# Row maxima one step later, reciprocals two steps behind the scores, and low parts and half sums late in a step: an attention block on one core

## The chip, the cores and the metric

The kernel runs on one core of one Trainium2 chip. The metric is device time in microseconds. The kernel before was timed in three runs, with a median of 973.12 us (972.27 to 975.09).

## The reference

One layer of a streaming encoder, for a sequence of 1024 rows with 1024 features, all in float32. Two attention branches with 8 heads each share one input projection; each branch's output is gated, projected, merged with a sigmoid gate and sent through an output projection. The heart of each branch is the same: scores, a causal mask, softmax over the keys, times V.

```python
# branch A, 8 heads: 64 features + 32 rotary features, mask by chunks of 64 keys
for i in range(seq // Q_BLOCK):               # Q_BLOCK = 128 rows
    lo, hi = i * Q_BLOCK, (i + 1) * Q_BLOCK
    s = (q_nope[lo:hi] . k_nope[:hi] + q_rope[lo:hi] . k_rope[:hi]) * scale
    s = jnp.where(chunk_causal_mask(lo, hi), s, -jnp.inf)
    p = jax.nn.softmax(s, axis=-1)
    outs.append(p @ v[:hi])
# branch B, 8 heads of 64: the same with cum[lo:hi] - cum[:hi] added, mask by single keys
y_a = o_a * jax.nn.silu(gate_a)
y_b = o_b * jax.nn.silu(gate_b)
merged = (sigmoid(mg_a) * (y_a @ w_branch_a) + sigmoid(mg_b) * (y_b @ w_branch_b))
x = x + gate * (merged @ w_out)
```

## The kernel before

The kernel is one program with a written order for each engine; nothing reorders it at run time. A float32 product is made of a high part (float32r, by a cast on ScalarE) and a low part (the difference, by VectorE), so each matmul is three or two passes over high and low operands. This is why so much of VectorE's work is subtraction: of P, of weights, of Q and K.

The first 260 us project the input. Then comes `attention()`, from about 286 to 816 us: 16 heads, eight of branch A and eight of branch B, each in 12 steps of nominally 2.49 us (`STEP`). Step k of a head is one pair (g, j): g is the half of the 1024 queries (4 row tiles of 128 each), j the tile of 128 keys; k below 4 is (0, k), the others are (1, k - 4). In a step:

- `turn` transposes the blocks of the normalised P that belong to keys j into a "t" bank of PSUM (two buffers). ScalarE copies the high part out of it, VectorE subtracts the low part (`pp` in the traces).
- ScalarE computes the exp of the score tile that was made a step ago (`p_h` for a tile of the first half, `p_u` for one of the second).
- In some steps (0, 3, 5, 6 and 10 of even heads, 3 of odd ones) Q or K of the next two heads is transposed into a "t" bank (`qt`, `kt`) and written as high and low operands (`prep_a`, `prep_b`).
- `scores` makes the scores of row tile i of a coming head (the table `ahead` says which), in bank "n" for i below 4 and bank "s" for the others. Each has one buffer. VectorE puts the mask on (a memset of a 64 x 64 corner in branch A, an addition in branch B) and takes the negated row maximum `nm`.
- VectorE takes the reciprocal `rs` of the sum of the last exp, and GpSimd multiplies P by it.
- `fill_to` issues matmuls of an independent product, the gates' projections of the input (`f` in the traces), until the step has its length. Their evacuation (a tanh on ScalarE, a combined add and multiply on VectorE, `gate`) and the splitting of the next weights (two casts on ScalarE, two low parts `lo_f` on VectorE) are issued where the fill comes to them. Then the products P V of the last step (`o`), and after a head's half the two halves of o are added (`op`), gated on GpSimd and stored.

So each engine's queue is a list, and the code's order in a step is the order in each queue. Once, at step 0 of head 3, `gate_row` adds `gcol` on VectorE, and PE transposes it at once (`pgT`).

The order of issue in a step of the kernel before:

```python
pr = self.turn(n, g, j)              # transposes, high part, low part
if last: next(last)                  # exp of the last score tile
if (n, k) in parts: next(preps[parts[n, k]])
if k in ahead and ...: finish = self.scores(...)   # scores, mask, row maximum
if last: next(last)                  # reciprocal, multiply
...
self.fill_to(due - 600)              # fill, and its evacuations
```

Of the kernel before, what the change touches and what calls it, by code (L numbers as in the profile page):

```python
# [10 lines left out]
F32 = mybir.dt.float32  # L11
# [4 lines left out]
ALU = mybir.AluOpType  # L16
# [3 lines left out]
P = 128  # L20
# [54 lines left out]
class Net:  # L75
# [954 lines left out]
    def prep_a(self, n):  # L1030

        nc, U = self.nc, self.U
        h = self.seq[n][1]
        cols = slice(h * 64, h * 64 + P)
        ops = {}

        def load(nm, dram):
            src = U.get([P, ST, P], F32, f"{nm}s{n}")
            nc.sync.dma_start(src, dram[:, :, cols].rearrange("s p d -> p s d"))
            return src  # L1040

        def operands(nm):
            for e in range(2):
                ops[nm, e] = U.get([P, S], F32R, f"{nm}1_{n + e}"), U.get([P, S], F32R, f"{nm}2_{n + e}")
                r = (h + e) % 4 * 32
                for j, x in enumerate(ops[nm, e]):
                    nc.sync.dma_start(x[64:96].bitcast(F32),
                                      self.qr_d[j, (h + e) // 4, r:r + 32] if nm == "q" else self.kr_d[j])

        def group(nm, src, vec, g):  # L1050
            pt = self.bank("t", f"{nm}t{n}{g}")
            for i in range(4):
                self.transpose(pt[:, i * P:(i + 1) * P], src[:, g * 4 + i])
            sl = slice(g * 512, (g + 1) * 512)
            own = (slice(0, 64), slice(64, 128))
            for e in range(2):
                nc.scalar.activation(ops[nm, e][0][0:64, sl], pt[own[e]], AF.Copy, scale=vec[own[e]])
            for e in range(2):
                nc.vector.scalar_tensor_tensor(out=ops[nm, e][1][0:64, sl], in0=pt[own[e]], scalar=vec[own[e]],
                                               in1=ops[nm, e][0][0:64, sl].bitcast(F32), op0=ALU.mult, op1=ALU.subtract)  # L1060
            if g == 1:
                U.put(src)

        src = load("q", self.qa_d)
        yield
        operands("q")
        group("q", src, self.vqa, 0)
        yield
        group("q", src, self.vqa, 1)
        yield  # L1070
        src = load("k", self.ka_d)
        yield
        operands("k")
        group("k", src, self.vka, 0)
        for e in range(2):
            self.qk[n + e] = [*ops["q", e], *ops["k", e]]
            qh, ql, kh, kl = (x[0:96] for x in self.qk[n + e])
            self.passes[n + e] = [(qh, kh), (qh, kl), (ql, kh)]
        yield
        group("k", src, self.vka, 1)  # L1080
        yield

    def prep_b(self, n):
# [17 lines left out]
        def group(nm, src, vec, g):  # L1101
            pt = self.bank("t", f"{nm}t{n}{g}")
            for i in range(4):
                self.transpose(pt[:, i * P:(i + 1) * P], src[:, g * 4 + i])
            sl = slice(g * 512, (g + 1) * 512)
            own = (slice(0, 64), slice(64, 128))
            for e in range(2):
                nc.scalar.activation(x1[nm, e][own[e], sl], pt[own[e]], AF.Copy, scale=vec[own[e]])
            for e in range(2):
                hi = x1[nm, e][own[e], sl].bitcast(F32)  # L1110

                lo, again = (x2[nm, e][0:64, sl], x1[nm, e][own[1 - e], sl])[::1 if nm == "q" else -1]
                nc.vector.scalar_tensor_tensor(out=lo, in0=pt[own[e]], scalar=vec[own[e]], in1=hi,
                                               op0=ALU.mult, op1=ALU.subtract)
                nc.gpsimd.tensor_scalar(out=again, in0=hi, scalar1=1.0, scalar2=0.0, op0=ALU.mult, op1=ALU.add)
            if g == 1:
                U.put(src)

# [24 lines left out]
    def scores(self, n, i):  # L1143
# [14 lines left out]
        if i == 7:  # L1158
            self.U.put(*self.qk.pop(n))
        sv = s[:, base:base + w]  # L1160
        if br == "b":
            nc.vector.tensor_tensor(out=sv[:, w - P:w], in0=sv[:, w - P:w], in1=self.maskb, op=ALU.add)
        else:
            nc.vector.memset(sv[0:64, w - 64:w], NEG)
        nm = pa.tile([P, 1], F32, tag="nm", bufs=4, name=f"nm{n}_{i}")
        nc.vector.tensor_reduce(out=nm, in_=sv, axis=AX.X, op=ALU.max, negate=True)  # L1166
        p = self.Hs.get([P, 512], F32, f"p{n}_{i}") if i < 4 else self.U.get([P, S], F32, f"p{n}_{i}")
        self.p[n, i] = p

        def finish():  # L1170
            sm = pa.tile([P, 1], F32, tag="sm", bufs=4, name=f"sm{n}_{i}")
            nc.scalar.activation(p[:, 0:w], sv, AF.Exp, bias=nm, accum_out=sm)  # L1172
            yield
            rs = pa.tile([P, 1], F32, tag="rs", bufs=4, name=f"rs{n}_{i}")
            nc.vector.reciprocal(rs, sm)  # L1175
            nc.gpsimd.tensor_scalar(out=p[:, 0:w], in0=p[:, 0:w], scalar1=rs, scalar2=0.0, op0=ALU.mult, op1=ALU.add)  # L1176
            yield
        return finish()

    def turn(self, n, g, j):  # L1180
# [9 lines left out]
        pp = self.U.get([P, 2, 512], F32R, f"pp{n}_{g}{j}")  # L1190
        ph, pl = pp[:, 0], pp[:, 1]
        nc.scalar.copy(ph[:, c0:], pt[:, c0:])  # L1192
        nc.vector.tensor_tensor(out=pl[:, c0:], in0=pt[:, c0:], in1=ph[:, c0:].bitcast(F32), op=ALU.subtract)  # L1193

        def product():
            v = self.v[n]
# [13 lines left out]
            nc.scalar.copy(tmp[0:64], o[64:128])  # L1210
            if n % 2 == 0 and g == 0:
                self.opair = self.U.get([P, S], F32, f"op{n}")
            r0 = (n % 2) * 64
            sl = slice(g * 512, (g + 1) * 512)
            op = self.opair[:, sl]
# [2 lines left out]
            if n % 2 == 1:  # L1218
# [9 lines left out]
                else:  # L1228
# [5 lines left out]
                        nc.scalar.copy(hi[:, sl], op)  # L1234
                        nc.vector.tensor_tensor(out=lo[:, sl], in0=op, in1=hi[:, sl].bitcast(F32), op=ALU.subtract)
                    self.U.put(self.opair, gate)
        return product

    def attention(self):
        N = len(self.seq)  # L1240
# [14 lines left out]
        for c, i in enumerate((0, 4, 1, 5, 2, 3, 6)):  # L1255
            if c == 3:
                self.load_v(1)
            if c == 4:
                while not self.g1b_done:
                    next(self.fill)  # L1260
                self.fbanks = "fg"
            if finish:
                next(finish)
            f = self.scores(0, i)
            if finish:
                next(finish)
            finish = f
            self.fill_to(self.pe_time + 1500)
        due = self.pe_time
        ahead = {1: (0, 7), 2: (1, 0), 4: (1, 1), 6: (1, 2), 8: (1, 3), 7: (1, 4), 9: (1, 5), 11: (1, 6)}  # L1270
        for n in range(N):
            for k in range(12):
                g, j = (0, k) if k < 4 else (1, k - 4)
                due += self.STEP
                pr = self.turn(n, g, j)
                last, finish = finish, None
                if last:
                    next(last)
                if (n, k) in parts:
                    next(preps[parts[n, k]])  # L1280
                if k in ahead and n + ahead[k][0] < N:
                    finish = self.scores(n + ahead[k][0], ahead[k][1])
                if last:
                    next(last)
                if k == 2 and 0 < n < N - 1:
                    self.load_v(n + 1)
                for at, call, a in self.extra:
# [46 lines left out]
    def build(self):  # L1334
# [26 lines left out]
        self.pending, self.pending_b = (), ()  # L1361
        self.seq = [("a", h) for h in range(H)] + [("b", h) for h in range(H)]
        self.passes, self.qk, self.v, self.p, self.gates, self.y, self.wo = {}, {}, {}, {}, {}, {}, {}
        self.extra = []
        for k in range(2):
            self.extra += [((14, 1), self.load_y, (0, k)), ((14, 3), self.split_y, (0, k)),
                           ((14, 4), self.load_y, (0, 2 + k)), ((14, 6 + k), self.split_y, (0, 2 + k)),
# [127 lines left out]
```

## Time and profile before

| | |
|---|---|
| median of three runs | 973.12 us (972.27 to 975.09) |
| profiled execution | 970.98 us, of which the span is 969.0 |
| TensorE busy | 952.2 us (98%) |
| VectorE busy | 636.0 us (66%) |
| ScalarE busy | 477.6 us (49%) |
| GpSimd busy | 204.0 us (21%) |
| DMA | 39.3% of 16 engines' span, 124 MB |

The share of TensorE says that there is next to no time in which it does not work; the share of the others says that they have time on the whole, but not at which moment. TensorE's clock is the other thing to read: the profile gives the clock granted to it, 1.00 for 2.4 GHz and 0.50 for 1.2 GHz. How the engines' queues meet has to be read from the timeline of single steps.

### The profile page before, as it was taken

The page shows a single profiled execution, that of the slowest core. Times are in us where ns is not written, and L with a number is a line of the kernel's source. Part 1 is how long each engine was busy: PE and PEld are TensorE (multiplying, and loading weights), DVE is VectorE, ACT ScalarE, POOL GpSimd, SP SyncE. Part 2 cuts the span into 40 slices and gives each one's busy share as a digit, 9 for nine tenths or more (in the row PEclk, how much of TensorE's full clock was granted, in tenths as well). Part 3 has the DMA queues.
Part 4 walks back from the last instruction along what each step waited for, and adds up shares of the span by engine and source line. Part 5 has one row for each costly group of instructions (what it writes and reads, how often), then busy time and mean ns, then how long its engine had stood idle before and what let it go on. Part 6 is the DMA issues. An engine that isn't in the chain of part 4 may idle for free.

```text
span 969.0 us, 15332 instructions
## 1 busy us (share of the span) xinstructions
PE 952.2 (98%) x5582; PEld 832.3 (86%) x5582; DVE 636.0 (66%) x1379; ACT 477.6 (49%) x959; POOL 204.0 (21%) x260
## 2 busy tenths in 40 slices
PE   7999999999999999999999999999999999999998
PEld 7999999999988888788888888888888878887887
DVE  3967977787646667567667676677676766596222
ACT  7776634443245656546555566465655644143000
POOL 0022132200011222122233233232332220045000
PEclk9999999999999999999999999999999999999999
DMA  9821132864943224225232232322411554633321
GB/s 348 322 95 45 50 116 81 295 225 169 312 134 98 87 67 131 66 74 155 79 109 67 66 90 67 114 85 88 132 56 44 185 185 153 245 141 125 109 88 66
DMA packets 80987, 124.99 MB, mean 129 GB/s; under 512 B 5928, under 2 KB 47536, under 8 KB 80912
## 3 DMA queue, kind: packets, MB, share of 16 engines
q1 hardware_dynamic: 80912, 124.01, 39.3%
q8 instruction: 44, 0.72, 0.3%
q14 instruction: 31, 0.25, 0.1%
HBM read 88.33 MB, written 35.66 MB: 128 GB/s over the span
## 4 chain that ended last, share of the span: by engine, by line
PE 89%; DVE 4%; DMA 3%; ACT 2%; issue 2%; POOL 0%; SPq 0%; ACTq 0%; DVEq 0%
PE f L127 31%; PE b L127 12%; PE out L127 9%; PE s L127 9%; PE o L127 7%; PE pt L136 6%; PE q L127 3%; PE ckv L127 2%; PE kv L127 2%; PE cq_s L127 2%; DVE hT_lo L998 1%; DMA ks_u<-ka_d 1%; PE cq_t L127 1%; DVE mg_h L991 1%; PE pada L127 1%
## 5 line engine op out<-in xcount | busy, mean ns | idle before, releaser
L1192 ACT CAST pp_u<-pt 128x512 fp32r<-128x512 f32 x192 | 92.2, 480 | 178.9 <-PE pt L136 164.9
L1193 DVE TENSOR_TENSOR pp_u<-pt,pp_u 128x512 fp32r<-128x512 f32 x192 | 106.5, 555 | 76.5 <-ACT pp_u L1192 74.4
L127 PE MATMUL f<-hT_hi,hi_f_u 128*128 128x512 f32 x384 | 153.9, 401 | 0.0
L127 PE MATMUL f<-hT_lo,hi_f_u 128*128 128x512 f32 x384 | 153.7, 400 | 0.0
L127 PE MATMUL f<-hT_hi,lo_f_u 128*128 128x512 f32 x384 | 153.5, 400 | 0.0
L127 PE MATMUL s<-k_u,q_u 96*128 96x512 f32 (+6 forms) x480 | 117.1, 363 | 1.2 <-ACT p_h L1172 0.7
L127 PE MATMUL b<-hi_b_u,hT_hi 128*128 128x256 f32 x384 | 109.6, 286 | 0.0
L127 PE MATMUL b<-hi_b_u,hT_lo 128*128 128x256 f32 x384 | 108.6, 283 | 0.0
L127 PE MATMUL b<-lo_b_u,hT_hi 128*128 128x256 f32 x384 | 108.6, 283 | 0.0
L1176 POOL TENSOR_SCALAR p_u<-p_u,rs 128x640 f32<-128x640 f32 (+1 forms) x64 | 64.7, 1011 | 169.1 <-DVE rs L1175 93.2
L1166 DVE TENSOR_REDUCE nm<-s 128x1 f32<-128x128 f32 (+7 forms) x128 | 97.0, 758 | 4.4
L127 PE MATMUL o<-pp_u,v_u 128*128 128x512 f32 (+7 forms) x384 | 94.4, 340 | 0.0
L1176 POOL TENSOR_SCALAR p_h<-p_h,rs 128x128 f32<-128x128 f32 (+1 forms) x64 | 36.9, 577 | 249.3 <-DVE rs L1175 220.0
L127 PEld LDWEIGHTS s<-k_u,q_u 96*128 96x128 f32 (+2 forms) x480 | 77.1, 191 | 7.0 <-ACT p_h L1172 1.2
L127 PEld LDWEIGHTS f<-hT_hi,lo_f_u 128*128 128x128 f32 x384 | 72.5, 189 | 12.0
L127 PEld LDWEIGHTS f<-hT_hi,hi_f_u 128*128 128x128 f32 x384 | 72.7, 189 | 11.1
L127 PEld LDWEIGHTS f<-hT_lo,hi_f_u 128*128 128x128 f32 x384 | 72.5, 189 | 11.2
L127 PEld LDWEIGHTS o<-pp_u,v_u 128*128 128x128 f32 (+1 forms) x384 | 62.0, 162 | 19.7 <-issue 0.2
L127 PEld LDWEIGHTS b<-lo_b_u,hT_hi 128*128 128x128 f32 x384 | 73.6, 192 | 0.3
L127 PEld LDWEIGHTS b<-hi_b_u,hT_hi 128*128 128x128 f32 x384 | 73.6, 192 | 0.3
L127 PEld LDWEIGHTS b<-hi_b_u,hT_lo 128*128 128x128 f32 x384 | 73.6, 192 | 0.0
L136 PEld LDWEIGHTS pt<-ident,p_u 128*128 128x128 f32 x416 | 52.7, 140 | 16.7
(310 smaller groups left out, 1998.5 us busy)
## 6 DMA issues: line engine op xcount, KB each, us to landing
raw_f_u<-in_w_t SPq DMA_DIRECT2D x24, 512.0 KB
wada_u<-in_w_ada SPq DMA_DIRECT2D x16, 512.0 KB
mg_d<-th_h SPq DMA_DIRECT2D x32, 256.0 KB
mg_h<-mg_d SPq DMA_DIRECT2D x32, 256.0 KB
raw_b_u<-in_w_b SPq DMA_DIRECT2D x12, 512.0 KB
x_u<-in_x SPq DMA_DIRECT2D x8, 512.0 KB
raw_wg_u<-in_w_gate SPq DMA_DIRECT2D x8, 512.0 KB
va_d<-vhl_u SPq DMA_DIRECT2D x8, 512.0 KB
```

Source lines behind the costliest of these rows:

```text
L127: self.nc.tensor.matmul(out, lhsT=l, rhs=r, start=start, stop=stop)
L136: self.nc.tensor.transpose(out=out, in_=in_, identity=self.ident)
L991: nc.vector.scalar_tensor_tensor(out=m, in0=m, scalar=1.0, in1=acc, op0=ALU.add, op1=ALU.mult)
L998: nc.vector.tensor_tensor(out=self.hT_lo[x], in0=mA[c1][:, x[2]], in1=self.hT_hi[x].bitcast(F32), op=ALU.subtract)
L1166: nc.vector.tensor_reduce(out=nm, in_=sv, axis=AX.X, op=ALU.max, negate=True)
L1176: nc.gpsimd.tensor_scalar(out=p[:, 0:w], in0=p[:, 0:w], scalar1=rs, scalar2=0.0, op0=ALU.mult, op1=ALU.add)
L1192: nc.scalar.copy(ph[:, c0:], pt[:, c0:])
L1193: nc.vector.tensor_tensor(out=pl[:, c0:], in0=pt[:, c0:], in1=ph[:, c0:].bitcast(F32), op=ALU.subtract)
```

## The change

Three of the pieces of VectorE's work in a step move. The mask and the row maximum go from `scores` to the beginning of the next step, ahead of that step's low part of P. The reciprocal and GpSimd's multiply go two steps behind the scores. The low parts of the operands of later heads (and GpSimd's copies with them) and the sum of the halves of o are collected in a list, `late`, and issued behind the reciprocal, the latter one step after its product.

```diff
@@ prep_a (prep_b alike, with its copies on GpSimd)
-            for e in range(2):
-                nc.vector.scalar_tensor_tensor(out=ops[nm, e][1][0:64, sl], in0=pt[own[e]], scalar=vec[own[e]],
-                                               in1=ops[nm, e][0][0:64, sl].bitcast(F32), op0=ALU.mult, op1=ALU.subtract)
+
+            def lows():
+                for e in range(2):
+                    nc.vector.scalar_tensor_tensor(out=ops[nm, e][1][0:64, sl], in0=pt[own[e]], scalar=vec[own[e]],
+                                                   in1=ops[nm, e][0][0:64, sl].bitcast(F32), op0=ALU.mult, op1=ALU.subtract)
+
+            if n == 0:
+                lows()
+            else:
+                self.late.append(lows)
...
@@ scores
         sv = s[:, base:base + w]
-        if br == "b":
-            nc.vector.tensor_tensor(out=sv[:, w - P:w], in0=sv[:, w - P:w], in1=self.maskb, op=ALU.add)
-        else:
-            nc.vector.memset(sv[0:64, w - 64:w], NEG)
-        nm = pa.tile([P, 1], F32, tag="nm", bufs=4, name=f"nm{n}_{i}")
-        nc.vector.tensor_reduce(out=nm, in_=sv, axis=AX.X, op=ALU.max, negate=True)
...
         def finish():
+            if br == "b":
+                nc.vector.tensor_tensor(out=sv[:, w - P:w], in0=sv[:, w - P:w], in1=self.maskb, op=ALU.add)
+            else:
+                nc.vector.memset(sv[0:64, w - 64:w], NEG)
+            nm = pa.tile([P, 1], F32, tag="nm", bufs=4, name=f"nm{n}_{i}")
+            nc.vector.tensor_reduce(out=nm, in_=sv, axis=AX.X, op=ALU.max, negate=True)
+            yield
             sm = pa.tile([P, 1], F32, tag="sm", bufs=4, name=f"sm{n}_{i}")
             nc.scalar.activation(p[:, 0:w], sv, AF.Exp, bias=nm, accum_out=sm)
             yield
@@ turn
-        nc.vector.tensor_tensor(out=pl[:, c0:], in0=pt[:, c0:], in1=ph[:, c0:].bitcast(F32), op=ALU.subtract)
+
+        def low():
+            nc.vector.tensor_tensor(out=pl[:, c0:], in0=pt[:, c0:], in1=ph[:, c0:].bitcast(F32), op=ALU.subtract)
...
+            if n < 15:
+                self.late.append(lambda: collect(o, tmp))
+            else:
+                collect(o, tmp)
+
+        def collect(o, tmp):
             r0 = (n % 2) * 64
...
-        return product
+        return low, product
@@ attention
+        last, opening = None, True
         for n in range(N):
             for k in range(12):
                 g, j = (0, k) if k < 4 else (1, k - 4)
                 due += self.STEP
-                pr = self.turn(n, g, j)
-                last, finish = finish, None
+                older, last, finish = last, finish, None
+                if last and not opening:
+                    next(last)
+                low, pr = self.turn(n, g, j)
+                low()
                 if last:
                     next(last)
                 if (n, k) in parts:
                     next(preps[parts[n, k]])
                 if k in ahead and n + ahead[k][0] < N:
                     finish = self.scores(n + ahead[k][0], ahead[k][1])
-                if last:
-                    next(last)
+                if older:
+                    next(older)
+                opening = False
+                while self.late:
+                    self.late.pop(0)()
```

What this does to the queues: the order on PE, ACT, POOL and SP is the same in both kernels, and on DVE it changes throughout the attention. Three places show how. In the names, `pp7_17` is the part of P of head 7 for half 1 and key tile 7, `s8_6` and `nm8_6` the scores and the row maximum of tile 6 of head 8, `rs8_5` a reciprocal, `lo_f13` the low parts of a weight of the fill, `gate4` an evacuation of the fill. The numbers behind them are buffers.

The first place is VectorE's queue at the end of head 7 and the first two steps of head 8, in the kernel before:

```order
L1175 RECIPROCAL rs8_5_6478<-sm8_5_6476 128x1
L1193 TENSOR_TENSOR pp7_17_u26_386_6494<-pt7_17_6492,pp7_17_u26_386_6494 128x128
L1162 TENSOR_TENSOR s8_6_6497<-s8_6_6497,maskb_105 128x128
L1166 TENSOR_REDUCE nm8_6_6503<-s8_6_6497 128x1
L978 SCALAR_TENSOR_TENSOR gate4_u8_388_6512<-th120_h0_142_6510,f12_00_6433 128x512
L116 TENSOR_TENSOR lo_f13_u23_390_6515<-raw_f13_u27_382_6431,hi_f13_u7_389_6514 128x512 x2
L1193 TENSOR_TENSOR pp8_00_u28_391_6531<-pt8_00_6526,pp8_00_u28_391_6531 128x512
L1175 RECIPROCAL rs8_6_6538<-sm8_6_6534 128x1
```

The same place in the changed kernel:

```order
L1207 TENSOR_TENSOR pp7_17_u21_386_6491<-pt7_17_6489,pp7_17_u21_386_6491 128x128
L1187 RECIPROCAL rs8_5_6500<-sm8_5_6473 128x1
L978 SCALAR_TENSOR_TENSOR gate4_u8_388_6509<-th120_h0_142_6507,f12_00_6427 128x512
L116 TENSOR_TENSOR lo_f13_u23_390_6512<-raw_f13_u27_382_6425,hi_f13_u7_389_6511 128x512 x2
L1177 TENSOR_TENSOR s8_6_6494<-s8_6_6494,maskb_105 128x128
L1181 TENSOR_REDUCE nm8_6_6524<-s8_6_6494 128x1
L1207 TENSOR_TENSOR pp8_00_u28_391_6531<-pt8_00_6526,pp8_00_u28_391_6531 128x512
L1207 TENSOR_TENSOR pp8_01_u2_393_6555<-pt8_01_6551,pp8_01_u2_393_6555 128x384
```

Mask and row maximum of tile 6 stood ahead of the fill's gate and low parts and now stand behind them; the reciprocal of tile 5 went behind the low part of its step.

The second place is VectorE's queue in steps 8 to 10 of head 9, in the kernel before:

```order
L1162 TENSOR_TENSOR s10_3_7144<-s10_3_7144,maskb_105 128x128
L1166 TENSOR_REDUCE nm10_3_7148<-s10_3_7144 128x1
L1175 RECIPROCAL rs10_4_7151<-sm10_4_7142 128x1
L978 SCALAR_TENSOR_TENSOR gate5_u13_438_7164<-th150_h7_160_7162,f15_00_7071 128x512
L1193 TENSOR_TENSOR pp9_15_u3_439_7170<-pt9_15_7166,pp9_15_u3_439_7170 128x384
L1162 TENSOR_TENSOR s10_5_7175<-s10_5_7175,maskb_105 128x128
L1166 TENSOR_REDUCE nm10_5_7181<-s10_5_7175 128x1
L1175 RECIPROCAL rs10_3_7184<-sm10_3_7173 128x1
L116 TENSOR_TENSOR lo_f16_u10_442_7188<-raw_f16_u14_433_7069,hi_f16_u28_441_7187 128x512 x2
L1193 TENSOR_TENSOR pp9_16_u16_443_7204<-pt9_16_7201,pp9_16_u16_443_7204 128x256
L1175 RECIPROCAL rs10_5_7209<-sm10_5_7207 128x1
```

The same place in the changed kernel:

```order
L978 SCALAR_TENSOR_TENSOR gate5_u3_438_7158<-th150_h2_160_7156,f15_00_7068 128x512
L1177 TENSOR_TENSOR s10_3_7141<-s10_3_7141,maskb_105 128x128
L1181 TENSOR_REDUCE nm10_3_7161<-s10_3_7141 128x1
L1207 TENSOR_TENSOR pp9_15_u1_439_7167<-pt9_15_7163,pp9_15_u1_439_7167 128x384
L1187 RECIPROCAL rs10_4_7178<-sm10_4_7139 128x1
L116 TENSOR_TENSOR lo_f16_u18_442_7182<-raw_f16_u14_433_7066,hi_f16_u28_441_7181 128x512 x2
L1177 TENSOR_TENSOR s10_5_7172<-s10_5_7172,maskb_105 128x128
L1181 TENSOR_REDUCE nm10_5_7196<-s10_5_7172 128x1
L1207 TENSOR_TENSOR pp9_16_u10_443_7201<-pt9_16_7198,pp9_16_u10_443_7201 128x256
L1187 RECIPROCAL rs10_3_7206<-sm10_3_7170 128x1
```

The row maximum of tile 3 went behind the gate, that of tile 5 behind the pair of low parts of the weight f16.

The third place is VectorE's queue at step 0 of head 3, where `gate_row` is, in the kernel before:

```order
L1193 TENSOR_TENSOR pp2_17_u9_255_4704<-pt2_17_4702,pp2_17_u9_255_4704 128x128
L1164 MEMSET s3_6_4707 64x64
L1166 TENSOR_REDUCE nm3_6_4715<-s3_6_4707 128x1
L1193 TENSOR_TENSOR pp3_00_u6_257_4729<-pt3_00_4724,pp3_00_u6_257_4729 128x512
L1175 RECIPROCAL rs3_6_4734<-sm3_6_4732 128x1
L897 TENSOR_TENSOR gcol_113<-gcol_113,vec_91 128x8
```

The same place in the changed kernel:

```order
L1207 TENSOR_TENSOR pp2_17_u9_255_4701<-pt2_17_4699,pp2_17_u9_255_4701 128x128
L1187 RECIPROCAL rs3_5_4712<-sm3_5_4667 128x1
L1179 MEMSET s3_6_4704 64x64
L1181 TENSOR_REDUCE nm3_6_4722<-s3_6_4704 128x1
L1207 TENSOR_TENSOR pp3_00_u6_257_4729<-pt3_00_4724,pp3_00_u6_257_4729 128x512
L897 TENSOR_TENSOR gcol_113<-gcol_113,vec_91 128x8
```

The reciprocal of tile 6 is no longer in front of `gcol`; that of tile 5 comes in its place, ahead of the row maximum.

## Rows read from the trace of the kernel before

**Rows 1.** The page: busy us and share of the span of each engine.

```profile
PE 952.2 (98%) x5582; PEld 832.3 (86%) x5582; DVE 636.0 (66%) x1379; ACT 477.6 (49%) x959; POOL 204.0 (21%) x260
```

**Rows 2.** Waits of PE, 300 to 816 us: us in total, times, longest.

```profile
PE pgT L136 <- DVE gcol L897: 2.4, 1, 2.4
PE s L127 <- ACT p_u L1172: 0.5, 1, 0.5
PE qt L136 <- DVE pp_u L1193: 0.2, 1, 0.2
```

**Rows 3.** Windows: busy us (count) PE, PEld, DVE, ACT, POOL; PEclk; DMA; GB/s.

```profile
395.50:398.91 3.41, 3.41 (x13) 2.61 (x12) 0.74 (x2) 1.66 (x3) 0.00 (x0) 0.50 0.87 214
875.00:885.00 10.00, 8.32 (x38) 6.55 (x37) 7.98 (x12) 6.01 (x11) 4.35 (x4) 1.00 0.30 109
```

**Rows 4.** Timeline (start us, length us, engine), heads 7 and 8, 555 to 560.

```profile
555.42 1.09 DVE L1166 TENSOR_REDUCE nm<-s 128x1 f32<-128x896 f32 x1
...
557.31 1.29 DVE L116 TENSOR_TENSOR lo_f_u<-raw_f_u,hi_f_u 128x512 fp32r<-128x512 f32 x2
...
558.07 1.02 ACT L1172 ACTIVATE p_u<-s,nm 128x896 f32<-128x896 f32 x1
...
559.71 0.48 PE L127 MATMUL s<-k_u,q_u 128*128 128x512 f32 x1
```

**Rows 5.** Timeline, head 9, steps 8 to 11.

```profile
614.05 0.69 DVE L978 SCALAR_TENSOR_TENSOR gate_u<-th_h,f 128x512 f32<-128x512 f32 x1 [0.69 <-ACT th_h L974]
...
614.27 0.70 ACT L1172 ACTIVATE p_h<-s,nm 128x512 f32<-128x512 f32 x1
...
614.95 1.15 ACT L115 CAST hi_f_u<-raw_f_u 128x512 fp32r<-128x512 f32 x2
...
615.12 0.29 DVE L1162 TENSOR_TENSOR s<-s,maskb 128x128 f32<-128x128 f32 x1
...
615.45 0.96 DVE L1166 TENSOR_REDUCE nm<-s 128x1 f32<-128x768 f32 x1
...
616.53 0.91 ACT L1172 ACTIVATE p_u<-s,nm 128x768 f32<-128x768 f32 x1
...
618.47 1.07 PE L127 MATMUL s<-k_u,q_u 128*128 128x512 f32 x4
```

**Rows 6.** Timeline, head 4, steps 8 to 10.

```profile
451.28 0.69 DVE L1166 TENSOR_REDUCE nm<-s 128x1 f32<-128x512 f32 x1
...
452.20 1.31 POOL L1176 TENSOR_SCALAR p_u<-p_u,rs 128x640 f32<-128x640 f32 x1 [1.46 <-PE o L127]
...
452.22 1.82 DVE L116 TENSOR_TENSOR lo_f_u<-raw_f_u,hi_f_u 128x512 fp32r<-128x512 f32 x2 [0.18 <-ACT hi_f_u L115]
...
453.97 0.55 DVE L1193 TENSOR_TENSOR pp_u<-pt,pp_u 128x384 fp32r<-128x384 f32 x1
...
454.68 0.38 PE L136 MATMUL kt<-ident,ks_u 128*128 128x128 f32 x2
```

**Rows 7.** Timeline, head 9, steps 1 to 3.

```profile
593.33 1.23 DVE L1166 TENSOR_REDUCE nm<-s 128x1 f32<-128x1024 f32 x1
...
595.47 1.29 DVE L116 TENSOR_TENSOR lo_f_u<-raw_f_u,hi_f_u 128x512 fp32r<-128x512 f32 x2 [0.91 <-ACT hi_f_u L115]
...
596.68 0.42 DVE L1193 TENSOR_TENSOR pp_u<-pt,pp_u 128x256 fp32r<-128x256 f32 x1
...
597.35 0.60 PE L136 MATMUL kt<-ident,ks_u 128*128 128x128 f32 x4
```

**Rows 8.** Timeline, DVE, head 3, step 0.

```profile
393.83 0.16 DVE L1175 RECIPROCAL rs<-sm 128x1 f32<-128x1 f32 x1 [0.64 <-ACT p_u L1172]
```

**Rows 9.** Timeline, head 4, steps 2 to 4.

```profile
436.77 0.29 DVE L1193 TENSOR_TENSOR pp_u<-pt,pp_u 128x128 fp32r<-128x128 f32 x1
...
437.00 1.14 POOL L1176 TENSOR_SCALAR p_u<-p_u,rs 128x1024 f32<-128x1024 f32 x1 [2.33 <-DVE rs L1175]
...
438.52 0.60 PE L136 MATMUL pt<-ident,p_u 128*128 128x128 f32 x4
```

More of the change, by code (lines that the diff above doesn't have):

```diff
@@ L1108, in group, with lows @@
                 nc.scalar.activation(x1[nm, e][own[e], sl], pt[own[e]], AF.Copy, scale=vec[own[e]])
[L1109 to L1115, printed above, removed]
+            def lows():
+                for e in range(2):
+                    hi = x1[nm, e][own[e], sl].bitcast(F32)
+                    lo, again = (x2[nm, e][0:64, sl], x1[nm, e][own[1 - e], sl])[::1 if nm == "q" else -1]
+                    nc.vector.scalar_tensor_tensor(out=lo, in0=pt[own[e]], scalar=vec[own[e]], in1=hi,
+                                                   op0=ALU.mult, op1=ALU.subtract)
+                    nc.gpsimd.tensor_scalar(out=again, in0=hi, scalar1=1.0, scalar2=0.0, op0=ALU.mult, op1=ALU.add)
+            self.late.append(lows)
             if g == 1:
@@ L1264, in attention @@
             f = self.scores(0, i)
+            next(f)
             if finish:
@@ L1363, in build @@
         self.passes, self.qk, self.v, self.p, self.gates, self.y, self.wo = {}, {}, {}, {}, {}, {}, {}
-        self.extra = []
+        self.extra, self.late = [], []
         for k in range(2):
```

## The prediction

> **What bounds the kernel now.** I read the page first: TensorE is busy 952.2 of 969.0 us, VectorE 66%, ScalarE 49%, GpSimd 21% [rows 1]. So only two things count: where PE waits, and where its clock falls. The waits of PE over the attention stretch (300 to 816 us, all that the change touches but the last store) come to 3.1 us in three places [rows 2]: 2.4 us for `gcol`, 0.5 for an exp, 0.2 for a low part. Behind the first one the granted clock reads 0.50 (1.2 GHz) for 3.41 us before it is back at 1.00 (2.4 GHz) [rows 3]; at half speed that costs half of it, 1.7 us. So the prize is at most 3.1 + 1.7 = 4.8 us. There is nothing else to win: every other PE wait in that stretch is zero. On the losing side PE has no slack of its own: whatever newly delays it is added to the end.
>
> PE runs in a written order: each step's transposes, scores, fill, products. Three PSUM resources tie it to VectorE: the score bank ("n" for tiles 0 to 3, "s" for 4 to 7, one buffer each) comes free when the exp has read it, and the exp needs the row maximum; a "t" bank (two buffers) comes free when the low part has been subtracted; and the transposes of tile i need the normalised P, which needs the reciprocal. So I look for places where a DVE instruction in front of one of these now waits for something that it did not wait for.
>
> **What the change moves.** PE, ACT, POOL and SP keep their order; only DVE's queue changes. No instruction is added or removed, so there is no cost by count: everything is in what stands in front of what.
>
> *The row maximum.* It used to be issued right behind its scores, ahead of that step's fill. Now it is first in the next step, ahead of the low part, but behind all that the fill of its own step put on DVE: the evacuation of a fill bank, 0.69 us, and the two low parts of a weight split, 1.29 us, which themselves wait for ScalarE's casts [rows 4, 5]. In most steps no such thing is in the fill and the exp has room. Where it is, I re-lay the chain by hand from the rows' own starts and lengths. A handover from one engine to the next is 0.12 us (reduce ends 616.41, exp starts 616.53 [rows 5]); a mask takes 0.33 from its start to the reduce's [rows 5].
>
> 1. *Step 11 of head 7.* Before, the reduce ran at 555.42, ahead of the gate and the pair of low parts, and the exp at 558.07 to 559.09, in time for the scores that reuse "s" at 559.71 [rows 4]. Now the pair ends about 558.5, then mask 0.33 and reduce 1.09 to 559.9, exp 1.02 to 561.05, and a handover: PE starts at 561.15 in place of 559.71. Loss **1.45**. Head 10 has the same pattern at its step 11, re-laid in the same way: **1.4**.
>
> 2. *Steps 8 to 11 of head 9.* Two delays add up. The gate ends at 614.65, then mask .33 and reduce 0.69 (the length of a 512-wide one [rows 6]) to 615.67, and exp at 615.8 where it was 614.27. ScalarE's hi casts stand behind it (start to start 0.68, length 1.15): they end 617.6, not 616.1, the second low part at 618.3. Only then come mask .33 and reduce 0.96, 619.6, and exp 0.91, 620.6. The scores that want the bank are at 618.47 [rows 5]. Loss **2.1**. Head 14's steps 6 to 8 repeat it with the splits of y: **1.6**.
>
> 3. *Step 1 of head 9.* The reduce of tile 7, 1.23, ran in the gap before the pair at 595.47. Now it starts behind the pair (596.68 plus .33) and ends 598.24; the low part, 0.42, ends 598.65. `kt` at 597.35 takes that "t" bank [rows 7]. Loss **1.3**. Head 12's step 1 has the same with `qt`: 0.35 if the pair runs alone there, about 1.3 more if a multiply on GpSimd lands beside it (one is 1.31 [rows 6]); I take **0.9**, about the middle, since neither row decides.
>
> 4. *Step 8 of heads 2, 4, 6 and 12.* Low part of step 9 ends 454.52, `kt` at 454.68 wants its bank: no slack behind a handover. The reduce, 0.69 at 451.28, and a memset were ahead of the pair and now stand between pair and low part: +0.75 [rows 6]. But the pair is 1.82 there, beside GpSimd's normalising multiply of 1.31, which starts 0.02 before it [rows 6], against 1.29 with GpSimd elsewhere [rows 4]. That multiply now comes one step later (next part), so I take the pair at 1.29: +0.25. Four places: **1.0**, with 3.0 as the upper bound. The Trainium skill ("SBUF — State Buffer", "SBUF: two separate sides") says that a VectorE instruction with two SBUF inputs and a GpSimd one that reads SBUF exclude each other for a whole instruction, so that a collision costs what is left of the other. The trace agrees in sign, 0.53 more [rows 6], though a full exclusion of 1.31 would make it more. By the rule, moving the multiply takes the collision away and this term is 1.0; without it, 3.0.
>
> 5. *Steps 2 to 4 of head 8:* a gate now stands ahead of a reduce, a low part, a reciprocal and the multiply on GpSimd, hence of a transpose. It can cost at most the gate's 0.69 [rows 4] less a handover, 0.6, and at least a tenth, since this chain has next to no room; I take **0.4**.
>
> Losses: 1.45 + 1.4 + 2.1 + 1.6 + 1.3 + 0.9 + 1.0 + 0.4 = **10.15 us**.
>
> *Reciprocal two steps behind.* It frees DVE from one wait a step: at 393.19 DVE stood 0.64 us for the exp before the reciprocal, and `gcol` stood right behind it [rows 8]. That is a gain, costed below. What it delays is the transpose of P. Tile 7 is tightest: its exp is at step 2, its reciprocal is now at step 3 behind the low part, and the first transposes at step 4. In head 4 the low part of step 3 starts 436.77 and takes 0.29, then reciprocal 0.17 and multiply 1.14: with a handover of 0.12 on either side about 438.4, against the transposes at 438.52 [rows 9]. It just fits: nothing, unless DVE is later (rival below).
>
> *Low parts of the operands late in the step; o's halves a step later.* Their readers are whole steps off, and PE has not been kept waiting by any of them for more than 0.2 [rows 2]: nothing either way. What they do take off is work in front of reciprocals: the 0.2 and the 0.5 of [rows 2], of which I give back **0.3**.
>
> *`gcol`.* With the reciprocal gone it follows the low part at once, 0.64 earlier [rows 8]. The reduce that now stands behind its step's fill and ahead of that low part takes, I guess, 0.15 of it, so **0.5** is gained of the 2.4. Does the clock still fall? The wait would be about 1.8. In the stretch from 875 to 885 PE is busy 8.32 of 10.00 us, because of one wait of 1.7 for `mg_h` at 877.6, and the clock reads 1.00 throughout [rows 3], so I take it that the fall disappears, **1.7** (bounds: 0 and 1.7; I put the odds at two in three).
>
> **Sum.** 10.15 − 0.5 − 1.7 − 0.3 = +7.65. The profiled execution took 970.98 us (span 969.0), 2.14 below the median of the three runs, 973.12. So 978.6 for such an execution and **980.8 us** as a median, 0.8% slower. Its own range: all bounds low (item 3 0.35, item 5 0.1, items 1 and 2 a third smaller, since each hangs on starts that I read to a tenth and on fill that shifts) gives about +4.5, 977.5; all high (3.0, 1.6, 0.6, no clock gain) +12.2, 985.5.
>
> **Rivals.** *(a) It is faster.* The row maximum's place costs nothing, because exp had room: in [rows 5] exp ends 617.44 and its bank is wanted at 618.47, 1.0 us of slack. If gates and pairs run so early in their steps that each reduce slips less than that slack, only the gains stay: 0.9 of `gcol`, 1.7 of clock, 0.2 and 0.5, so 973.12 − 3.3 = 969.8. It decides at a slip of 1.0; against it is that a pair alone is 1.29 and waits for casts besides. *(b) No change.* Half the losses are given back: PE's wait in one step lets DVE catch up before the next, so that neighbouring places share one stall, and the gains eat the rest; about 973 to 975.5. Against it: the places lie heads apart, and PE has no wait from 816 on that is a transfer's and could swallow lateness, except the 1.7 at 877.6. *(c) Worse, by tile 7.* If in step 3 DVE or GpSimd is 0.2 to 0.4 us later than in [rows 9], the transposes of step 4 wait in each head whose slack is small. I count nine heads of 16 with 0.14 to 0.20: 9 × 0.15 to 0.25 is another 1.3 to 2.3, 982 to 983; at 0.5 late in all 16 (0.35 each) another 5.6, 986.4. For it: the whole chain is serial and fits by a tenth.
>
> **Chances.** As forecast (977.5 to 985.5) 0.66; (c) beyond that range or at its upper end 0.14; (b) 0.13; (a) 0.07. A measurement of this kernel tells 0.3%, 2.9 us, from no change: faster is below 970.2, slower above 976.0. Nearly all of the forecast and of (c) is slower, and a little of (b) may be: 0.81; same 0.13; faster 0.06. The range leaves out (a), the lower part of (b), and the top of (c): **975.0 to 986.5**.
>
> **What the profile after should show.** Waits of PE for an exp (`p_u`, `p_h`) at scores of steps 9 to 11 and 0 to 1 of heads 7 to 11 and 14, about 6.5 us in total; waits of `kt` and `qt` for a low part, about 3; `gcol` 1.7 to 1.9 and no clock of 0.50 behind it; PE's order unchanged. If transposes `pt` wait for the multiply in every head, (c) is right. I am wrong if scores wait less than 3 us in total: then the fill's work on DVE was not in front of the row maxima for as long as I re-laid it. I am also wrong if new clock falls follow the waits of 1.4 to 2.1 us: each could cost as much as the one of [rows 3].

## The result and the profile after

The changed kernel takes 981.9 us as the median of four runs (980.14 to 983.65), 1.0086 times the kernel before, with a 95% interval of 1.0057 to 1.0116. Slower, as forecast, and within 1.1 us of the 980.8 predicted. Ratios here and below compare fast executions alone; one slow one of the kernel before (1172.23 us) and one of e3 (1989.47 us) are left out.

The profiled execution of the changed kernel took 983.65 us (span 981.9). Its page, first line of the engines:

```profile
PE 954.7 (97%) x5582; PEld 831.0 (85%) x5582; DVE 627.5 (64%) x1379; ACT 478.3 (49%) x959; POOL 200.6 (20%) x260
```

Same instructions, and VectorE is even busy for less time than in [rows 1]; most of what grew is PE's waiting. The waits of PE from 285 to 860 us (the view of [rows 2], over a longer stretch):

```profile
PE s L127 <- ACT p_u L1184: 5.9, 5, 2.0
PE s L127 <- ACT p_h L1184: 1.6, 3, 0.8
PE pgT L136 <- DVE gcol L897: 1.6, 1, 1.6
PE qt L136 <- DVE pp_u L1207: 1.5, 2, 1.3
PE kt L136 <- DVE pp_u L1207: 1.3, 2, 1.1
PE pt L136 <- POOL p_u L1188: 0.4, 1, 0.4
PE pt L136 <- POOL p_h L1188: 0.3, 1, 0.3
```

The last line and 0.7 of the `p_h` line lie ahead of 300 us, and the kernel before has them too. The scores' other waits for an exp, 6.8 us, are nearly all where the forecast has them (0.5 is the wait of [rows 2]), so are those of `kt` and `qt` for low parts, and `gcol` waits 1.6 in place of 2.4. Behind that wait the clock stays at 1.00, where it read 0.50 in [rows 3] (windows of the changed kernel, columns as there):

```profile
396.40:400.00 3.60, 3.60 (x19) 2.97 (x20) 0.41 (x2) 2.03 (x5) 0.00 (x0) 1.00 0.47 122
```

The first place of the forecast, head 7 to 8, can be laid beside [rows 4] row by row (timeline of the changed kernel):

```profile
558.40 1.28 DVE L116 TENSOR_TENSOR lo_f_u<-raw_f_u,hi_f_u 128x512 fp32r<-128x512 f32 x2
...
559.93 1.09 DVE L1181 TENSOR_REDUCE nm<-s 128x1 f32<-128x896 f32 x1
...
561.11 1.01 ACT L1184 ACTIVATE p_u<-s,nm 128x896 f32<-128x896 f32 x1 [1.83 <-DVE nm L1181]
...
562.26 0.50 PE L127 MATMUL s<-k_u,q_u 128*128 128x512 f32 x1 [1.16 <-ACT p_u L1184]
```

The mask (at 559.60) and the reduce come when the pair of low parts ends, the exp starts 0.09 behind the reduce's end, PE 0.14 behind the exp's: the chain in the order in which the forecast laid it.

**Place by place.** PE executes the same 5582 instructions in the same order in all kernels here. So the n-th instruction of one trace can be paired with the n-th of another, and the difference of their starts followed along the program: where it jumps, time was lost or won. In this place, for instance, the scores stand at 559.71 before and 562.26 after, 2.55 apart, while some instructions ahead the pairs are about 1.1 apart: a jump of 1.4. The table gives these jumps against the trace of before, in us, worked out in this way from each kernel's trace (`kt` x4 sums four places; `front` is all up to 291 us, where the programs are the same; e1 to e11 are the experiments below).

| place | forecast | after | e1 | e2 | e6 | e10 | e11 |
|---|---|---|---|---|---|---|---|
| front | 0 | +2.7 | -0.6 | +0.7 | -0.7 | +4.3 | +2.1 |
| `gcol` | -0.5 | -0.8 | +0.1 | -0.9 | -0.9 | -0.8 | -0.9 |
| clock behind it | -1.7 | -1.6 | 0.0 | -1.6 | -1.6 | -1.6 | -1.6 |
| `kt` x4 | +1.0 | +1.1 | +1.3 | 0.0 | 0.0 | +1.1 | 0.0 |
| head 7, scores | +1.45 | +1.4 | +1.5 | 0.0 | +0.2 | +1.5 | 0.0 |
| head 8, `pt` | +0.4 | +0.7 | 0.0 | 0.0 | +0.7 | +0.1 | 0.0 |
| head 9, `kt` | +1.3 | +1.3 | +1.3 | +0.1 | 0.0 | +1.3 | +0.1 |
| head 9, scores | +2.1 | +2.2 | +4.1 | 0.0 | +0.3 | +2.5 | 0.0 |
| head 10, scores | +1.4 | +1.4 | +1.4 | 0.0 | 0.0 | +1.4 | 0.0 |
| head 12, `qt` | +0.9 | +1.5 | +0.4 | +1.4 | +0.2 | +0.8 | 0.0 |
| head 14 | +1.6 | +3.2 | +1.3 | +2.3 | +2.9 | +1.3 | 0.0 |
| head 15, scores | 0 | 0.0 | +0.7 | +1.0 | -0.1 | +0.6 | +1.1 |
| attention, 291 to 800 | +7.65 | +10.6 | +18.5 | +2.8 | +1.4 | +9.7 | -1.5 |

The front is no part of the change. There the transposes of the first K wait for a load, 2.7 us in this execution and 1.6 in that of before, with a lower clock behind the longer one; this wait differs from run to run (last section). That is why the two profiled executions are 12.7 us apart and the medians less. The place in head 15 is its first scores, which wait 0.5 us for an exp before the change as well. The mask and the reduce in front of this exp stand behind the fill's pair of low parts, whose casts wait for the load of their weight: 3.8 us from the load's issue to the first cast before, 4.5 in the changed kernel and 5.5 in e11. No run shows why this time differs, so I do not count the place for or against a piece of the change.

### The profile page after: what moved, and what is told of

It reads as the page before. It is cut to its first block, busy times and chain, and to the rows that moved or that the text cites. A ratio compares the mean times of both kernels' runs of the same rounds, so it can differ in the third digit from the quotient of the medians.

```text
span 981.9 us, 15302 instructions
## 1 busy us (share of the span) xinstructions
PE 954.7 (97%) x5582; PEld 831.0 (85%) x5582; DVE 627.5 (64%) x1379; ACT 478.3 (49%) x959; POOL 200.6 (20%) x260
## 4 chain that ended last, share of the span: by engine, by line
PE 82%; DVE 7%; DMA 4%; ACT 3%; issue 3%; POOL 0%; SPq 0%; ACTq 0%; POOLq 0%
PE f L127 27%; PE b L127 12%; PE out L127 9%; PE s L127 8%; PE o L127 6%; PE pt L136 6%; PE q L127 3%; PE ckv L127 2%; PE kv L127 2%; PE cq_s L127 2%; DVE lo_f_u L116 1%; DVE nm L1181 1%; DVE hT_lo L998 1%; DMA ks_u<-ka_d 1%; PE cq_t L127 1%
## 5 line engine op out<-in xcount | busy, mean ns | idle before, releaser
L1188 POOL TENSOR_SCALAR p_u<-p_u,rs 128x640 f32<-128x640 f32 (+1 forms) x64 | 61.8, 966 | 199.9 <-DVE rs L1187 107.6
L1184 ACT ACTIVATE p_u<-s,nm 128x640 f32<-128x640 f32 (+1 forms) x64 | 61.4, 960 | 28.8 <-DVE nm L1181 28.7
```

## The experiments

All ratios are to the kernel before, run on the same chip beside it, with 95% intervals.

**e1: the row maximum alone.** From the changed kernel, reciprocal and late work back at their places:

```diff
-                if older:
-                    next(older)
+                if last:
+                    next(last)
...
-                self.late.append(lows)
+                lows()
...
-                self.late.append(lambda: collect(o, tmp))
+                collect(o, tmp)
```

> Only the row maximum goes one step later; reciprocal, operands' low parts and half sums stay where they were before. My theory (the row maximum behind the fill's gate and low parts makes the losses): every wait of PE for an exp at the scores and for a low part at kt and qt is there as in the changed kernel, about 12 us in heads 4 to 14; the reciprocal stands ahead of gcol again, so its wait is 2.4 to 3 us and the clock falls behind it; the 0.4 us wait of a transpose for GpSimd in head 8 may go. Time 982.5 to 984.5. Rival (the reciprocal two steps behind or the late low parts make a good part of it): 975 to 979, with fewer waits of scores.

Measured: 1.016 [1.0136, 1.0185], median 989.0. The places in the table are there as expected, the clock falls behind `gcol`, and some 5 us more are lost than I thought. Two things make them. Head 9's scores wait 2.4 us here, and behind that wait the clock reads 0.50 for 3.41 us, which takes the place from 2.2 to 4.1. And about 6 us go in some twenty pieces of 0.1 to 0.4 that the table leaves out; heads 8, 12 and 14 give back 3.6. What goes with the small pieces is seen in DVE's reciprocals, in the kernel before, in e1 and in the changed kernel (groups by line: busy us, mean ns, then the idle time in front of them and what ended it).

```profile
L1175 DVE RECIPROCAL rs<-sm 128x1 f32<-128x1 f32 x128 | 20.3, 159 | 19.4 <-ACT p_u L1172 18.4
```

```profile
L1184 DVE RECIPROCAL rs<-sm 128x1 f32<-128x1 f32 x128 | 20.9, 164 | 40.6 <-ACT p_u L1181 33.1 <-ACT p_h L1181 5.1
```

```profile
L1187 DVE RECIPROCAL rs<-sm 128x1 f32<-128x1 f32 x128 | 19.6, 153 | 0.0
```

With a late maximum the exp is late, and a reciprocal one step behind the scores stands still for it: 40.6 us of DVE's queue held up, against 19.4 before and none after the change. So the late maximum costs more alone than in company. That the reciprocal's standing still makes the small pieces is argued from these rows and not shown: the late maximum with the late reciprocal and nothing else was not run.

**e2: the row maximum back, the rest as changed.**

```diff
-                if last and not opening:
-                    next(last)
...
                     finish = self.scores(n + ahead[k][0], ahead[k][1])
+                    next(finish)
```

> The changed kernel with the row maximum back in the step of its scores, ahead of the fill; reciprocal two steps behind, low parts and half sums late as changed. My theory: no wait for an exp at scores but those of before, none for a low part over 0.3, gcol waits 1.5 to 1.8 in place of 2.4 and no clock of 0.50 behind it: 970 to 971.5, 2 to 3 us below before. Rival (the late reciprocal makes transposes wait for GpSimd in many heads): 975 to 980.

Measured: 1.0023 [1.0005, 1.0041]. The waits for exps in heads 7, 9 and 10 and of all `kt` are gone, as the first theory had it, and `gcol` and the clock gain 2.5. But the time is not 2 to 3 us below before, as I expected: two losses stayed that I had given to the row maximum, `qt` in head 12 and most of head 14. They belong to the late half sum (e4, e11). Head 15 takes another 1.0.

**e3: the reciprocal alone.**

```diff
-                last, finish = finish, None
+                older, last, finish = last, finish, None
...
-                if last:
-                    next(last)
+                if older:
+                    next(older)
```

> The kernel before with the reciprocal and GpSimd's multiply two steps behind the scores, and nothing else changed. My theory: the same gain at gcol as in e2, 0.7 of the wait and the clock's 1.7, no new wait above 0.4: 970.5 to 972. Rival (transposes of tile 7 wait for the multiply): waits pt for POOL in many heads, 0.1 to 0.4 each, 974 to 978.

Measured: 1.0491 [1.0468, 1.0515], median 1022.06. The rival, and ten times its price. PE waits in the transposes of tile 7 at step 4 of 14 heads (waits of e3, then its timeline in head 4):

```profile
PE pt L136 <- POOL p_u L1176: 34.3, 14, 3.3
```

```profile
452.15 1.53 DVE L1059 SCALAR_TENSOR_TENSOR q_u<-qt,vqa,q_u 64x512 fp32r<-64x512 f32 x2 [1.34 <-ACT q_u L1057]
453.71 0.16 DVE L1175 RECIPROCAL rs<-sm 128x1 f32<-128x1 f32 x1
...
454.07 1.12 POOL L1176 TENSOR_SCALAR p_u<-p_u,rs 128x1024 f32<-128x1024 f32 x1 [3.93 <-DVE rs L1175]
...
455.25 0.33 PE L136 MATMUL pt<-ident,p_u 128*128 128x128 f32 x1 [2.49 <-POOL p_u L1176]
```

The low parts of `q_u` stand in front of the reciprocal; DVE waits 1.34 for ScalarE's cast before them, and they take 1.53. In the kernel before, the reciprocal of this tile comes a step earlier, ahead of them (timeline of [rows 9]; the second row is the first of the pair):

```profile
436.66 0.17 DVE L1175 RECIPROCAL rs<-sm 128x1 f32<-128x1 f32 x1 [0.63 <-ACT p_u L1172]
...
438.42 0.74 DVE L1059 SCALAR_TENSOR_TENSOR q_u<-qt,vqa,q_u 64x512 fp32r<-64x512 f32 x1 [1.35 <-ACT q_u L1057]
```

The 34.3 us and the clock, at 0.50 behind eight of the waits, make the 48.

**e6: the fill's low parts behind the row maximum.** The changed kernel, with one change of order on DVE (`split` puts its low parts into the list `splits`, which is also emptied ahead of the first product that reads them):

```diff
-                w[k + 1] = self.split(w[k + 1], f"f{k + 1}")
+                w[k + 1] = self.split(w[k + 1], f"f{k + 1}", later=self.splits if self.stepping else None)
...
+                while i == 0 and start and self.splits:
+                    self.splits.pop(0)()
...
+                while self.splits:
+                    self.splits.pop(0)()
                 low, pr = self.turn(n, g, j)
```

> The changed kernel, but the low parts of the fill's weight splits go behind the next step's row maximum in place of ahead of it; the splits of y in head 14 and 15 and the gates stay. My theory (it is what stands in front of the row maximum that counts): the exp waits in heads 7, 9 and 10 (1.2, 2.0 and 1.1 us) go or fall under 0.5 each, those in head 14 stay, and kt and qt keep their waits, since the low part of P is behind both either way: about 5 us less than the changed kernel, 976.5 to 978. Rival (one step later is too late for the exp by itself): exp waits stay, 981 to 982.5.

Measured: 1.0011 [0.9996, 1.0027], 7 us below the changed kernel. The exp waits of heads 7, 9 and 10 fall to 0.3 and less (table): a maximum taken a step later is harmless when the pair is not in front of it. I was wrong on `kt` and `qt`, which lost their waits too: with the pair behind the reduce, the order reduce, pair, low part is that of before, and it is this order that fits in. Head 14 keeps its 2.9, as the splits of y were not moved.

**e4: the late list alone.** From e2, the reciprocal one step behind as before:

```diff
-                older, last, finish = last, finish, None
+                last, finish = finish, None
...
-                if older:
-                    next(older)
+                if last:
+                    next(last)
```

> The kernel before with only the operands' low parts and the half sums of o late; row maximum in the step of its scores, reciprocal one step behind. Theory (the late half sum carries GpSimd's gate multiply beside the fill's low parts): the wait of qt in head 12, 1.2 to 1.4 in the changed kernel and in e2, is here too; gcol waits 2.4 and the clock falls, as before: 974.5 to 976. Rival (that wait comes from the late reciprocal or the row maximum): no wait of qt over 0.4, 972.5 to 973.5.

Measured: 1.0023 [1.0006, 1.004]. `qt` in head 12 waits 0.9 and jumps by 1.1, as the theory says, and head 14 loses 1.7. The timelines of e4 at head 12 and of the changed kernel there:

```profile
694.07 2.40 DVE L116 TENSOR_TENSOR lo_f_u<-raw_f_u,hi_f_u 128x512 fp32r<-128x512 f32 x2
694.13 1.79 POOL L1242 TENSOR_TENSOR op_u<-op_u,gate_u 128x512 f32<-128x512 f32 x1 [2.94 <-DVE op_u L1236]
```

```profile
699.98 1.77 POOL L1242 TENSOR_TENSOR op_u<-op_u,gate_u 128x512 f32<-128x512 f32 x1
700.51 1.78 DVE L116 TENSOR_TENSOR lo_f_u<-raw_f_u,hi_f_u 128x512 fp32r<-128x512 f32 x1
...
702.54 1.22 DVE L1181 TENSOR_REDUCE nm<-s 128x1 f32<-128x1024 f32 x1
```

The gate multiply, a step later than it was, lands on the pair of low parts: 2.40 for the pair, where [rows 4] has 1.29.

**e11: reciprocal and low parts late, half sums early.** e2, with `collect` right behind the product:

```diff
-                self.late.append(lambda: collect(o, tmp))
+                collect(o, tmp)
```

> e3 (reciprocal two steps behind, row maximum at its old place) with the low parts of the operands late, behind the reciprocal; half sums of o at their old place. Theory (in e3 the reciprocal stood behind these low parts at step 3 of every head, so making them late is what pays for the late reciprocal): the 14 waits of 2.2 to 3.3 us for GpSimd go, gcol waits 1.5 with no clock of 0.50 behind it, and qt in head 12 waits at most 0.4, as the half sum is not late: 970.5 to 972.5. Rival (it was the late half sum that made room in e2): several waits of pt for POOL stay, above 985.

Measured: 0.9975 [0.9957, 0.9992]. The waits of PE, 300 to 830 us:

```profile
PE pgT L136 <- DVE gcol L897: 1.5, 1, 1.5
PE s L127 <- ACT p_u L1184: 1.3, 1, 1.3
PE qt L136 <- DVE pp_u L1207: 0.2, 1, 0.2
```

No wait for GpSimd is left, so it is the operands' low parts that pay for the late reciprocal (e3 to e11: 50 us). The 1.3 is the wait in head 15. Head 12 and head 14 lose nothing, so their losses in e2 are the half sum's. How it acts in head 14 is seen on SP's queue and ScalarE (timelines of before, of e2 and of e11):

```profile
755.64 0.32 SPq L1223 DMA_DIRECT2D yb_d<-op_u  x1
756.38 0.82 SPq L102 DMA_DIRECT2D raw_y_u<-ya_d  x2
...
760.85 1.14 ACT L115 CAST hi_y_u<-raw_y_u 128x512 fp32r<-128x512 f32 x2 [1.10 <-DMA raw_y_u<-ya_d]
```

```profile
758.98 0.32 SPq L1243 DMA_DIRECT2D yb_d<-op_u  x1
759.39 0.88 SPq L102 DMA_DIRECT2D raw_y_u<-ya_d  x2
...
763.14 1.14 ACT L115 CAST hi_y_u<-raw_y_u 128x512 fp32r<-128x512 f32 x2 [3.11 <-DMA raw_y_u<-ya_d]
```

```profile
755.09 0.32 SPq L1240 DMA_DIRECT2D yb_d<-op_u  x1
755.83 0.82 SPq L102 DMA_DIRECT2D raw_y_u<-ya_d  x2
```

The loads of y stand behind the store of the gated o. With the half sum a step later the store is 3.3 us later, the loads 3.0, the casts of y 2.3, and their low parts meet the scores of head 14.

**e10: the changed kernel with early half sums.**

```diff
-            if n < 15:
-                self.late.append(lambda: collect(o, tmp))
-            else:
-                collect(o, tmp)
+            collect(o, tmp)
```

> The changed kernel with the half sums of o, the gate multiply and its store at their old place, right behind the product. Theory: head 12's wait of qt falls from 1.3 to 0.2 to 0.4, the exp waits in heads 7, 9 and 10 stay: 980 to 981. Rival (qt waits for the row maximum alone): qt keeps 1.0 or more and the time is that of the changed kernel.

Measured: 1.0093 [1.0066, 1.012], which overlaps that of the changed kernel: on time it says nothing. The table does: `qt` in head 12 falls from 1.5 to 0.8, head 14 from 3.2 to 1.3, head 8 from 0.7 to 0.1. Against these 3.2 us, about 2.2 are lost elsewhere: 0.3 more at head 9's scores, 0.6 in head 15, the rest in pieces of 0.1 to 0.3, which I did not follow up.

**e8: the splits of y behind the row maximum too.** On e6 (the lines that keep a product behind the low parts it reads are left out):

```diff
...
-        self.y[4 * br + k] = self.split(self.y[4 * br + k], f"y{br}{k}")
+        self.y[4 * br + k] = self.split(self.y[4 * br + k], f"y{br}{k}",
+                                        later=self.splits if br == 0 else None)
...
```

> As e6, with the low parts of the splits of y in head 14 behind the row maximum too. Theory: the exp waits in head 14 (2.8 us together in the changed kernel, 3 in e6) fall under 1; nothing else moves: 971 to 972.5. Rival (they come from the late half sum or the late reciprocal, since e2 has part of them with the row maximum at its old place): 974 to 975.

Measured: 1.0004 [0.998, 1.0027]: no measurable gain over e6. Head 14's jumps up to 776 us go from 2.9 to 0.9, but the place at the start of head 15 takes it back: a product waits 0.7 for a low part of P behind the fill's pair (it stands there in the kernel before too, but the weight's load takes 5.1 us to the first cast here), the next scores wait 1.3, and the clock reads 0.51 in the 3.5 us behind.

**e5, e12 and e13: `gcol` out of the way.** The addition goes to step 10 of head 2, in the kernel before (e5), in e11 (e12) and in e6 (e13):

```diff
+    def gate_add(self):
+        self.nc.vector.tensor_tensor(out=self.gcol, in0=self.gcol, in1=self.b_gate, op=ALU.add)
...
-        nc.vector.tensor_tensor(out=self.gcol, in0=self.gcol, in1=self.b_gate, op=ALU.add)
...
-        self.extra += [((3, 0), self.gate_row, ())]
+        self.extra += [((2, 10), self.gate_add, ()), ((3, 0), self.gate_row, ())]
```

> The kernel before with the one addition to gcol issued in step 10 of head 2 and not in step 0 of head 3; its transpose stays. Theory: the wait of 2.4 us is gone and no clock of 0.50 follows: 4.1 us less than before, 969 to 970. Rival (the clock falls anyhow there, or the time comes back as a wait behind): 971 to 973.

> e11 with gcol's addition in step 10 of head 2. Theory: what e5 has, as the reciprocal's place is worth nothing once gcol is out of its way: 969 to 971. Rival (the late reciprocal gives PE something of its own): below 968.

> e6 (the changed kernel with the fill's low parts behind the row maximum) with gcol's addition in step 10 of head 2. Theory: e6 less the 1.5 us that gcol still waits there, 972 to 973.5; 2 to 4 us above e5 because of head 14. Rival (e6 loses nothing but at gcol): as e5, 969 to 970.5.

Measured: e5 0.9955 [0.9938, 0.9972], median 969.76; e12 0.9966 [0.9949, 0.9984], median 969.97; e13 0.9999 [0.9977, 1.002]. In e5 all that PE still waits for between 300 and 830 us is this:

```profile
PE s L127 <- ACT p_u L1174: 0.8, 1, 0.8
PE qt L136 <- DVE pp_u L1195: 0.2, 1, 0.2
```

The paired starts give -2.6 for the wait and -1.6 for the clock. So the whole prize of the change, and more, is had by moving one small addition; with that done the late reciprocal brings nothing that can be measured (e12). e13, with maximum, reciprocal, low parts and half sums all late, still costs against e5, by its trace 2.7 in head 14. That is not the late maximum's alone: e2, with the maximum at its old place, loses 2.3 there. By time e5 and e12 can't be told apart; e5 is the smaller edit.

## Why the prediction was right, and where it was not

**The mechanism and its places: right.** The forecast said that the row maximum would stand behind the fill's gate and low parts, that the exp would be late where both are in the fill of a step, and named the places. Six of the eight terms came within 0.3 (table): heads 7, 9 and 10 at the scores, head 9's `kt`, the four `kt` of step 8, head 8's 0.7 against 0.4. e2 and e6 take the cause away in two ways, and the losses go; only head 8's stays in e6, where the gate still stands in front of the maximum, and it goes with early half sums (e10). That the late reciprocal would just fit behind the low part of step 3 [rows 9] held as well: one wait of 0.4 in all. The terms given for it add up to 438.6 and not to about 438.4, which is behind the first of the four transposes at 438.52; but it is the last of the four that reads tile 7. In the changed kernel it is 1.68 us from this low part's start (437.52) to the end of the multiply (439.20), and PE does not wait.

**`gcol` and the clock: right.** 0.5 forecast, 0.8 measured; 1.7 and 1.6 for the clock, which does not fall behind a wait of 1.6. The 0.3 that I gave back for [rows 2]'s other two waits was not there: 0.2 and 0.5 are waited for as before.

**The shared port: right, by a row of the trace after.** In step 8 of head 4 the pair takes 1.29 (and as much, within 0.02, in heads 2, 6 and 12), and `kt` waits 0.04:

```profile
452.87 1.29 DVE L116 TENSOR_TENSOR lo_f_u<-raw_f_u,hi_f_u 128x512 fp32r<-128x512 f32 x2 [1.02 <-ACT hi_f_u L115]
```

So it was GpSimd's multiply beside it that made it 1.82 in [rows 6]. The Trainium skill ("SBUF — State Buffer", "SBUF: two separate sides") has such a pair of instructions exclude each other for a whole instruction. At head 12 of the changed kernel the trace agrees: the low part that begins at 700.51 ends at 702.29, 0.54 behind the end of the multiply at 701.75, which is most of the 0.6 to 0.7 that it takes alone.

**The step that failed: "Low parts of the operands late in the step; o's halves a step later", put at "nothing either way".** For the half sums this was wrong. Their gate multiply lands on the fill's low parts in head 12 (+1.5 where I took 0.9, with 1.6 as the bound; that GpSimd might land there I had seen, but not which piece would), and their store stands in front of the loads of y on SP's queue, so that head 14 lost 3.2 and not 1.6. And in head 8 their addition stands in front of a row maximum (+0.7 with late half sums, +0.1 with early ones, e10). I had looked at who reads the sum and not at what else is in the queues that it passes; heads 12 and 14 together make 2.2 (0.6 and 1.6) of the 2.95 by which the attention came out above my sum (10.6 against 7.65). With the half sums early (e10) these two places cost 0.8 and 1.3, close to what I had put on the row maximum alone. For the low parts "nothing" was right of the sum and wrong of the reason: their lateness is worth some 50 us, the price of a late reciprocal without it.

**Why the median was still met.** The attention's 10.6 less the 0.5 that the paired starts regain from 870 us to the end would make 10.1; the ratio says 8.4 (5.5 to 11.3), by 973.12. The interval holds both, and the front's wait, which changes by more than this difference between executions, does not let me say more. By the traces the sum was 3 us too small, so that the median came within 1.1 us is partly luck.

## What to carry to other kernels

In a queue that is served in order, an instruction that moves a step later moves behind whatever that step's other work puts there; price it at the few places where that work is long, one by one, and not on average. Parts of one change can pay for each other: the late reciprocal alone cost 48 us, and with late low parts it won 2, all of it at `gcol`. Follow every queue that a moved piece passes, the stores on SP included, and look first for the single wait that holds the prize: here one addition of 0.15 us gave nearly all there was to win.

## What the runs showed of the hardware

The clock does not follow from a wait's length alone. In e3 two waits of 2.5 us of the same kind, in heads 3 and 4, were followed by different clocks (windows behind each):

```profile
419.38:422.79 3.41, 3.41 (x11) 2.51 (x10) 2.66 (x7) 2.52 (x5) 0.37 (x1) 0.50 0.00 0
455.25:459.00 3.75, 3.75 (x24) 3.26 (x25) 1.98 (x5) 1.70 (x3) 0.37 (x1) 1.00 1.07 294
```

In the traces here the clock fell behind 8 of the 14 waits of 2.2 to 3.3 us of e3, behind `gcol`'s 2.2, 2.4 and 2.5, and never behind its 1.5 or 1.6. Nor is there a length that parts the two: behind head 9's scores it fell after a wait of 2.4 us in e1 and not after one of 2.2 in e10, and in e8 it fell where waits of 0.7 and 1.3 us start 2 us apart.

The wait for the first K in the front is 0.7 us in one execution and 4.3 in another, with the same program up to there (e5, then e13; waits of PE, 260 to 290 us), and in the second the clock reads 0.51 for 6.9 us that begin inside the wait:

```profile
PE kt L136 <- DMA ks_u<-ka_d: 0.7, 1, 0.7
```

```profile
PE kt L146 <- DMA ks_u<-ka_d: 4.3, 1, 4.3
```

```profile
269.80:276.70 6.90, 4.61 (x22) 4.64 (x23) 1.80 (x3) 2.27 (x4) 0.00 (x0) 0.51 0.20 63
```

Up to the end of the front the traces here lie up to 6.1 us apart in this way (e12 to e13). That it makes most of the spread between executions of one kernel is likely but not shown, as each kernel has one trace. An issue of that load some steps earlier is what I would try next.
